# Summing the gate's four partial rows on VectorE, and issuing the queries' remainders one step later, in a one-core hybrid diffusion step

## The chip, the cores and the metric

The kernel runs on one core of a Trainium2 chip. The metric is the device time of one execution in microseconds (us). Beside the time there is a profile of one execution, taken by the hardware profiler, with a trace of every instruction.

Engines are named as in the profile: PE is TensorE (matrix products and transposes), PEld its weight loads, DVE is VectorE, ACT is ScalarE, POOL is GpSimd, SP is the engine that issues most transfers. ACT issues transfers too; in the trace those of ACT stand under ACTq, those of SP under SPq. Each engine runs its own instructions strictly in the order in which the program lists them, and waits at an instruction until all that it needs is there.

## The reference, cut to what matters

One layer of a diffusion backbone: 128 context tokens and 1024 latent tokens, width 1024. The part that the change touches is the modulation gate and the queries:

```
m = silu(cond) @ w_mod + b_mod          # cond: c for latent tokens, c_ctx for context tokens
shift, scale, gate = split(m, 3)
h = rmsnorm(x, norm_gain) * (1 + scale) + shift
q_a, k_a, v_a, g_a, q_b, k_b, v_b, g_b = split(h @ w_in)
q = rope(rmsnorm_per_head(q, qn))       # 8 heads of 64, for mixer A and for mixer B
... attention A (all keys), attention B (window of 128) ...
x = x + gate * (concat(o_a * silu(g_a), o_b * silu(g_b)) @ w_out)
```

The gate is a row of 1024 numbers for each of the two conditions. It is needed only at the very end, when the output projection is added to x.

## The kernel before, in words

All work is in tiles of 128 tokens; there are nine (the context tile is number 0). To keep fp32 accuracy, most operands are split into a high part, rounded for fast products, and a low part, the remainder (`whi`/`wlo` for weights, `qo0`/`qo1` for queries), and a product is done as three: high by high, low by high, high by low.

The order of the program is: modulation and gates of mixer A; queries of mixer A (nine blocks, `m = 0`); queries of mixer B (nine blocks, `m = 1`); keys and values (nine blocks); gates of mixer B; then attention and output, which fills the last two thirds of the time.

**A block and its steps.** A block (`block`, `project`, lines 244 to 281) is 24 products of 128x512 into one accumulation bank `pq` (or `pk` for keys): eight slices k of the width, three products each (lines 246, 247, 248, of which 247 uses the low weights `wlo`). Each block has two halves, and each half begins with a `tick()`, which runs the work that earlier blocks put in an agenda with `later(n, f)`: f runs n half blocks later. That is how the order of the work around the change is set: agenda entries of one tick run in the order in which they were put there, and every instruction then stands in its engine's list at that place.

**A query tile.** After its block, a tile goes through these steps (`query`, from line 614), at 0, 2, 3 and 6 ticks (`QUERY_AT`), for the last tile of mixer B at 0, 1, 2 and 4 (`QUERY_LAST`):

- squares: ACT squares `pq` (`sqq`, line 622), DVE sums (`ssq`, 624; `ms`, 169), POOL takes the power -1/2 (`rs`, 171);
- scale: DVE multiplies (`qnq`, 629) and makes the two rotary products (`ra`, 559; `rb`, 565);
- rotated: DVE adds them (`qfq`, 640; for tile 0 line 642);
- turned: PE transposes into a bank `ptq` (line 650; two such banks, D and E, used in turn by `bank_tr`), ACT makes the high part (`qo0q`, 653) and issues its two transfers to DRAM (`put`, 663);
- low, one tick later: DVE makes the low part (`qo1q`, 658);
- `put` of the low part, one further tick later: ACT issues two more transfers (663). There are two buffers each of `qo0` and `qo1`.

**The next weights.** During the last block of a stage, from its third slice on, the next stage's weights are split, one slice a time, the last two slices behind the block: ACT makes `whi` (line 231), DVE makes `wlo` (233). At the end of mixer A they are `whiqb`/`wloqb`, at the end of mixer B `whikv`/`wlokv`.

**The gate.** In two of mixer B's blocks (the tiles `GATE_AT`, 3 and 7 in order), `gate_rows` computes half of the gate, 512 columns: eight products over K, in four column groups of the array, so that the bank `pgate` holds four partial sums, at partitions 0, 32, 64 and 96, two rows each (one for each condition). Then ACT copies the bank to `grow` one tick later (line 604), and three ticks later `gate_sum` adds the four: PE multiplies `grow` by `sel`, a 128x2 matrix of ones and zeros, into a bank `pgs` of the D/E pair (line 593; the trace shows each such fp32 product as two), DVE adds the bias `bg` (594) and SP stores the row (595). `sel` is made once by `group_sum` (lines 320 and 322), which adds four column pairs of the identity.

Of the kernel before, what the change touches and what calls it, by code (L numbers as in the profile page):

```python
# [9 lines left out]
F32 = mybir.dt.float32  # L10
# [3 lines left out]
ALU = mybir.AluOpType  # L14
# [4 lines left out]
P = 128  # L19
# [32 lines left out]

WO_STEPS = ((0, 4, 4), (1, 5, 5), (2, 6), (3, 7), (4, 8, 6), (5, 9), (6, 11), (7, 12, 10), (8, 13), (9, 14), (10, 16))
TURN = 2
QUERY_AT = (0, 2, 3, 6)
PAD = 2
SECOND_FROM = 5
# [48 lines left out]
def hybrid_step(ctx, tc, x_prompt, x_sample, cache_k_a, cache_v_a, cache_k_b, cache_v_b,  # L106
# [3 lines left out]
    nc = tc.nc  # L110
# [13 lines left out]
    def later(n, f):  # L124

        agenda.setdefault(now[0] + n, []).append(f)
# [13 lines left out]
    def bank(tag, name):  # L140
        return ps.tile([P, 512], F32, tag=tag, name=name, bufs=BANKS[tag])

    def bank_mm(name):
        turn["mm"] += 1
        return bank(mm_tags[0][turn["mm"] % len(mm_tags[0])], name)

    def bank_tr(name):
        turn["tr"] += 1
        return bank("DE"[turn["tr"] % 2], name)
# [3 lines left out]
    ident_r = cst.tile([P, P], F32R, name="ident_r")  # L153
# [12 lines left out]
    def rsqrt_mean(pool, ss, n, width, name):  # L166

        ms = pool.tile([P, width], F32, tag="ms", name=f"ms_{name}")
        nc.vector.tensor_scalar(ms, ss, 1.0 / n, EPS, op0=ALU.mult, op1=ALU.add)  # L169
        r = pool.tile([P, width], F32, tag="rs", name=f"rs_{name}")  # L170
        nc.gpsimd.tensor_tensor(r, ms, mhalf[:, :width], op=ALU.pow)  # L171
        return r
# [136 lines left out]
    with tc.tile_pool(name="st", bufs=2, side="right") as st:  # L309
# [6 lines left out]
        nc.sync.dma_start(colt, cols)  # L316
        st.tile([P, 16], F32, name="pad3", bufs=1)

        def group_sum(out, eye):
            nc.vector.tensor_tensor(out, eye[:, 0:2], eye[:, 32:34], op=ALU.add)  # L320
            for a in (64, 96):
                nc.vector.tensor_tensor(out, out, eye[:, a : a + 2], op=ALU.add)

        wm = []

        def load_wm(j):
# [142 lines left out]
        for j in range(1, KT + 2):  # L469
# [54 lines left out]
            if KT - 2 <= j < KT:  # L524
# [3 lines left out]
                c0, n = W_QA.cols[0]  # L528
# [26 lines left out]
    def rope_products(pool, qn, nh, tab_c, tab_s, t, name, bufs=2):  # L555

        cb = tab_c[:, t - 1, :].unsqueeze(1).to_broadcast([P, nh, HD])
        ra = pool.tile([P, nh, HD], F32, tag="ra", name=f"ra_{name}", bufs=bufs)
        nc.vector.tensor_tensor(ra, qn, cb, op=ALU.mult)
        rb = pool.tile([P, nh, HD], F32, tag="rb", name=f"rb_{name}", bufs=bufs)  # L560
        rv = rb.rearrange("p h (b s f) -> p h b s f", s=2, f=16)
        qv = qn.rearrange("p h (b s f) -> p h b s f", s=2, f=16)
        sv = tab_s[:, t - 1, :].rearrange("p (b s f) -> p b s f", s=2, f=16)
        for s in range(2):
            nc.vector.tensor_tensor(rv[:, :, :, s, :], qv[:, :, :, 1 - s, :],
                                    sv[:, :, s, :].unsqueeze(1).to_broadcast([P, nh, 2, 16]), op=ALU.mult)
        return ra, rb
# [11 lines left out]
    with tc.tile_pool(name="qt", bufs=2, side="right") as qt:  # L579
# [4 lines left out]
        sil32 = qt.tile([P, KT, 32], F32, name="sil32g", bufs=1)  # L584
        nc.gpsimd.memset(sil32, 0.0)
        nc.vector.tensor_copy(sil32[:, :, 0:2], silc.rearrange("p (c k) -> p k c", c=2))
        sel = qt.tile([P, 2], F32, name="selg", bufs=1)
        group_sum(sel, ident_r.bitcast(F32))
        wg, bg = [], []

        def gate_sum(n, grow):
            pgs = bank_tr(f"pgs{n}")
            nc.tensor.matmul(pgs[0:2], sel, grow, start=True, stop=True)
            nc.vector.tensor_tensor(bg[n], pgs[0:2], bg[n], op=ALU.add)
            nc.sync.dma_start(gate_row[:, 512 * n : 512 * n + 512], bg[n])

        def gate_rows(n):
            pg = bank_mm(f"pgate{n}")
            for k in range(KT):
                a = 32 * (k % 4)  # L600
                nc.tensor.matmul(pg[a : a + 32], sil32[:, k, :], wg[2 * n + k // 4][:, k % 4, :],
                                 start=(k < 4), stop=(k >= 4), tile_position=(0, a))
            grow = qt.tile([P, 512], F32, tag="grow", name=f"grow{n}", bufs=1)
            later(1, lambda: nc.scalar.copy(grow, pg))
            later(3, lambda: gate_sum(n, grow))

        def load_wg(i):
            n, b = divmod(i, 2)
# [5 lines left out]
        def query(pq, m, t, tabs, n=1):  # L614

            nm = f"q{m}_{t}"
            pqv = pq.rearrange("p (h d) -> p h d", d=HD)
            v = {}

            def squares():  # L620
                sq = qt.tile([P, 8, HD], F32, tag="sq", name=f"sq{nm}")
                nc.scalar.activation(sq, pqv, AF.Square)  # L622
                ss = qt.tile([P, 8], F32, tag="ss", name=f"ss{nm}")
                nc.vector.tensor_reduce(ss, sq, axis=AX.X, op=ALU.add)
                v["r"] = rsqrt_mean(qt, ss, HD, 8, nm)

            def scale():
                qn = qt.tile([P, 8, HD], F32, tag="qn", name=f"qn{nm}")
                nc.vector.tensor_tensor(qn, pqv, v["r"].unsqueeze(2).to_broadcast([P, 8, HD]), op=ALU.mult)
                v["qn"] = qn  # L630
                if t:
                    v["rot"] = rope_products(qt, qn, 8, *tabs[m], t, nm)

            def rotated():

                qf = qt.tile([P, 4, 2, HD], F32, tag="qf", name=f"qf{nm}", bufs=3)
                out = qf.rearrange("p h g d -> p g h d")
                pair = lambda a: a.rearrange("p (g h) d -> p g h d", g=2)
                if t:
                    nc.vector.tensor_tensor(out, *(pair(a) for a in v["rot"]), op=ALU.add)  # L640
                else:
                    nc.vector.tensor_tensor(
                        out, pair(v["qn"]), gain4[:, 2 * m, :].unsqueeze(1).unsqueeze(1).to_broadcast([P, 2, 4, HD]),
                        op=ALU.mult)
                v["qf"] = qf

            def turned():
                ptq = bank_tr(f"pt{nm}")
                for h in range(4):
                    nc.tensor.transpose(ptq[:, P * h : P * h + P], v["qf"][:, h].rearrange("p g d -> p (g d)"),  # L650
                                        ident_r.bitcast(F32))
                qo = [qt.tile([P, 512], F32R, tag=f"qo{i}", name=f"qo{i}{nm}") for i in range(2)]
                nc.scalar.copy(qo[0], ptq)
                put(qo[0], 0)
                later(1, lambda: low(ptq, qo))

            def low(ptq, qo):
                nc.vector.tensor_tensor(qo[1], ptq, qo[0], op=ALU.subtract)
                later(1, lambda: put(qo[1], 1))

            def put(part, i):
                for g in range(2):
                    nc.scalar.dma_start(q_dram[t][m][64 * i : 64 * i + 64, 512 * g : 512 * g + 512],
                                       part[64 * g : 64 * g + 64].bitcast(F32))

            for d, f in zip(QUERY_LAST if (m, t) == (1, 0) else QUERY_AT, (squares, scale, rotated, turned)):
                later(n + d, f)

        tabs = {0: rope_tables(qt, 0, 2)}
        for m in range(2):  # L670
            w, nxt = ((W_QA, W_QB), (W_QB, W_KV))[m]
            ts = list(range(1, NT)) + [0]
            for t in ts:
                pq = bank_mm(f"pq{m}_{t}")
                if m == 1 and t in (ts[GATE_AT[0]], ts[GATE_AT[1]]):
                    gate_rows(len(wg) // 2 - 1)
                if (m, t) in ((0, ts[-2]), (1, ts[GATE_AT[0]])):
                    n = len(wg) // 2
                    load_wg(2 * n)
                    load_wg(2 * n + 1)  # L680
                    if n == 0:
                        bgt = qt.tile([34, 512], F32, name="bg", bufs=1)
                    bg.append(bgt[32 * n : 32 * n + 2])
                    nc.sync.dma_start(bg[n], b_mod[:, 2 * D + 512 * n : 2 * D + 512 * n + 512].to_broadcast([2, 512]))
                if t == ts[-2]:
                    nxt.load_all()
                    if m == 0:
                        tabs[1] = rope_tables(qt, 2, 2)
                block(pq, lambda k: project(pq, w, t, k), nxt, t == ts[-1])
                query(pq, m, t, tabs)  # L690
# [178 lines left out]
    def max_items(i):  # L869
# [19 lines left out]
        def finish():  # L889
# [10 lines left out]
            nc.vector.tensor_scalar(mn, m4, -1.0, None, op0=ALU.mult)  # L900
            later(TURN, transpose)

# [166 lines left out]
    for f in beside[2]:  # L1069
# [5 lines left out]
        name=nc.get_next_instruction_name(), engine=mybir.EngineType.Activation, act_func_set_id=6))  # L1075
# [155 lines left out]
    slots, start = [], []  # L1231
# [119 lines left out]
```

## Time and profile before

| | us |
|---|---|
| median of 3 timed runs | 716.38 (716.08 to 716.65) |
| the profiled execution, its own time | 716.94 |
| its span in the trace | 715.2 |
| PE busy | 694.4 (97%) |
| DVE busy | 463.8 (65%) |
| ACT busy | 416.4 (58%) |
| POOL busy | 334.6 (47%) |

The mean granted clock of TensorE was 0.994 of full speed. Times of events are counted from the start of the span; the execution's own time is 1.74 us more than the span, which lie around it. In the list of events in order of time, each row has the start, the time busy, engine, line, operation, what is written and read, shape and count; in brackets stands how long the engine had been idle before and what ended that. Time in which ACT issues transfers does not count as busy. Starts of products on PE lie closer together than their durations, since products overlap in the array: what a product costs is read from the distance of starts.

### The profile page before, as it was taken

The page shows a single profiled execution, that of the slowest core. Times are in us where ns is not written, and L with a number is a line of the kernel's source. Part 1 is how long each engine was busy: PE and PEld are TensorE (multiplying, and loading weights), DVE is VectorE, ACT ScalarE, POOL GpSimd, SP SyncE. Part 2 cuts the span into 40 slices and gives each one's busy share as a digit, 9 for nine tenths or more (in the row PEclk, how much of TensorE's full clock was granted, in tenths as well). Part 3 has the DMA queues.
Part 4 walks back from the last instruction along what each step waited for, and adds up shares of the span by engine and source line. Part 5 has one row for each costly group of instructions (what it writes and reads, how often), then busy time and mean ns, then how long its engine had stood idle before and what let it go on. Part 6 is the DMA issues. An engine that isn't in the chain of part 4 may idle for free. (4 is left out here: it accounts for less than half of the span.)

```text
span 715.2 us, 10633 instructions
## 1 busy us (share of the span) xinstructions
PE 694.4 (97%) x3512; PEld 559.1 (78%) x3512; DVE 463.8 (65%) x1016; ACT 416.4 (58%) x840; POOL 334.6 (47%) x356
## 2 busy tenths in 40 slices
PE   6999999999998999999999999999999999999987
PEld 4778988777686889976788888888888888887865
DVE  4767257866747864736867577567675775675662
ACT  5646411411414441178777877887788778877770
POOL 3647033232313320246757555755575557555651
PEclk9999999999999999999999999999999999999999
DMA  8962283358344026431222122122221221222323
GB/s 323 414 202 97 80 300 76 83 164 249 74 108 143 7 69 191 133 119 46 81 75 73 39 76 80 45 82 65 77 74 39 73 82 45 82 62 79 104 66 119
DMA packets 53304, 78.58 MB, mean 110 GB/s; under 512 B 6584, under 2 KB 25464, under 8 KB 52352
## 3 DMA queue, kind: packets, MB, share of 16 engines
q1 hardware_dynamic: 45072, 65.96, 28.0%
q10 hardware_dynamic: 8176, 11.94, 6.3%
q8 instruction: 28, 0.46, 0.3%
q14 instruction: 28, 0.23, 0.1%
HBM read 58.69 MB, written 19.18 MB: 109 GB/s over the span
## 5 line engine op out<-in xcount | busy, mean ns | idle before, releaser
L1136 POOL TENSOR_TENSOR pl<-pe,ph 128x512 fp32r<-128x512 f32 x130 | 167.7, 1292 | 145.4 <-DVE nm L947 67.6
L887 DVE TENSOR_REDUCE mx<-pmx 128x1 f32<-128x384 f32 x192 | 101.4, 552 | 60.2 <-PE pmx L886 58.9
L1128 ACT ACTIVATE pe<-st 128x512 f32<-128x512 f32 x146 | 86.9, 596 | 28.0 <-PE st L1126 27.0
L1132 ACT CAST ph<-pe 128x512 fp32r<-128x512 f32 x146 | 90.6, 620 | 4.8
L1146 PE MATMUL pv<-ph,v_hi 128*128 128x512 f32 x208 | 83.2, 400 | 2.2 <-DVE spare L1170 2.2
L1149 PE MATMUL pv<-pl,v_hi 128*128 128x512 f32 x208 | 82.5, 397 | 0.0
L171 POOL TENSOR_TENSOR rs_q<-ms_q,mhalf 128x8 f32<-128x8 f32 x18 | 34.8, 1931 | 82.2 <-DVE ms_q L169 82.2
L1217 PE MATMUL po<-wo,ogh 128*128 128x512 f32 x216 | 72.6, 395 | 0.2 <-DVE yt L1224 0.2
L947 DVE CUSTOM_DVE_ANT_0 sn<-sn,mask,nsink 128x512 f32<-128x512 f32 (+1 forms) x64 | 46.3, 724 | 38.4 <-PE sn L944 36.6
L886 PE MATMUL pmx<-kha,qt 128*128 128x384 f32 x192 | 60.9, 363 | 0.4 <-ACT pen L933 0.2
L1125 PE MATMUL st<-qt,kha 128*128 128x512 f32 x144 | 58.2, 404 | 1.5 <-ACT pe L1128 0.8
L1126 PE MATMUL st<-qb,kla 68*128 68x512 f32 x144 | 57.7, 401 | 1.1 <-DVE qb L906 1.1
L1148 PE MATMUL pv<-ph,v_lo 128*64 128x512 f32 x146 | 57.8, 396 | 0.0
L1149 PEld LDWEIGHTS pv<-pl,v_hi 128*128 128x128 f32 x208 | 39.3, 189 | 16.7 <-issue 0.4
L933 ACT ACTIVATE pen<-sn,nm 128x512 f32<-128x512 f32 (+2 forms) x72 | 45.1, 627 | 6.5 <-DVE nm L947 3.1
L1121 ACT CAST ph<-st 128x512 fp32r<-128x512 f32 x62 | 36.4, 588 | 19.9 <-PE st L1120 18.6
L1146 PEld LDWEIGHTS pv<-ph,v_hi 128*128 128x128 f32 x208 | 39.5, 190 | 10.7 <-ACT ogh L1182 2.4
L1217 PEld LDWEIGHTS po<-wo,ogh 128*128 128x128 f32 x216 | 39.9, 188 | 6.9 <-DVE yt L1224 0.6
L1122 DVE TENSOR_TENSOR pl<-st,ph 128x512 fp32r<-128x512 f32 x62 | 42.5, 686 | 2.1 <-ACT ph L1121 1.5
L1217 PE MATMUL po<-wo,ogl 128*128 128x512 f32 x108 | 42.5, 393 | 0.0
L622 ACT ACTIVATE sqq<-pq 128x512 f32<-128x512 f32 x18 | 10.8, 600 | 52.5 <-DMA qd<-qo0q 16.2
L886 PEld LDWEIGHTS pmx<-kha,qt 128*128 128x128 f32 x192 | 35.5, 190 | 6.3 <-DVE mx L887 1.4
(219 smaller groups left out, 1700.7 us busy)
## 6 DMA issues: line engine op xcount, KB each, us to landing
qt<-qd SPq DMA_DIRECT2D x36, 256.0 KB, 3.0
wm<-in_w_mod_ss_dram SPq DMA_DIRECT2D x7, 1024.0 KB, 10.0
qd<-qo0q ACTq DMA_DIRECT2D x36, 128.0 KB, 2.4
qd<-qo1q ACTq DMA_DIRECT2D x36, 128.0 KB, 2.4
sgl<-gd SPq DMA_DIRECT2D x36, 128.0 KB, 2.1
out_dram<-yt SPq DMA_DIRECT2D x17, 256.0 KB, 2.1
xn<-in_x_sample_dram SPq DMA_DIRECT2D x8, 512.0 KB, 6.1
wg<-in_w_mod_g_dram SPq DMA_DIRECT2D x4, 1024.0 KB, 8.4
```

Of the source, the lines that this page charges most:

```text
L886: nc.tensor.matmul(pm[:, 0:384], lhs, kha[:, g, 3 * b : 3 * b + 3, :], start=True, stop=True)
L887: nc.vector.tensor_reduce(mx[:, h, b : b + 1], pm[:, 0:384], axis=AX.X, op=ALU.max)
L947: nc.vector.tensor_tensor_reduce(s, s, mask[:, m0 : m0 + n], -1.0, nsink[:, 4 * g + h : 4 * g + h + 1], op0=ALU.add, op1=ALU.min, accum_ou ...
L1125: nc.tensor.matmul(s, kh, qtile[i], start=True, stop=False)
L1126: nc.tensor.matmul(s, kl, qbtile[i], start=False, stop=True)
L1128: nc.scalar.activation(pe, s, AF.Exp)
L1132: nc.scalar.copy(ph, pe)
L1136: nc.gpsimd.tensor_tensor(pl, pe, ph, op=ALU.subtract)
L1146: nc.tensor.matmul(pv, two, ph, start=(b == 0), stop=False)
L1148: nc.tensor.matmul(pv[0:64, :], vl, ph, start=False, stop=False)
L1149: nc.tensor.matmul(pv, two, pl, start=False, stop=last)
L1217: nc.tensor.matmul(po[n], a, wo_parts[KT * n + k][lo], start=(k == KS[0] and p == 0), stop=(k == KS[-1] and p == 2))
```

## The change

Two things. First, the product with `sel` goes, with `sel`, `grow`, ACT's copy and the extra bank: one tick after the gate's products, four DVE additions of 2x512 add the partial rows to the bias straight from the bank `pgate`, at partitions 0, 32, 64 and 96, each into `bg`. SP's store follows as before. Second, a new constant `PUT_LOW = 2` moves the transfers of a query's low part one tick later.

```
+PUT_LOW = 2
...
-        def group_sum(out, eye):
-            nc.vector.tensor_tensor(out, eye[:, 0:2], eye[:, 32:34], op=ALU.add)
-            for a in (64, 96):
-                nc.vector.tensor_tensor(out, out, eye[:, a : a + 2], op=ALU.add)
...
-        sel = qt.tile([P, 2], F32, name="selg", bufs=1)
-        group_sum(sel, ident_r.bitcast(F32))
         wg, bg = [], []

-        def gate_sum(n, grow):
-            pgs = bank_tr(f"pgs{n}")
-            nc.tensor.matmul(pgs[0:2], sel, grow, start=True, stop=True)
-            nc.vector.tensor_tensor(bg[n], pgs[0:2], bg[n], op=ALU.add)
+        def gate_sum(n, pg):
+            for a in range(0, P, 32):
+                nc.vector.tensor_tensor(bg[n], pg[a : a + 2], bg[n], op=ALU.add)
             nc.sync.dma_start(gate_row[:, 512 * n : 512 * n + 512], bg[n])
...
-            grow = qt.tile([P, 512], F32, tag="grow", name=f"grow{n}", bufs=1)
-            later(1, lambda: nc.scalar.copy(grow, pg))
-            later(3, lambda: gate_sum(n, grow))
+            later(1, lambda: gate_sum(n, pg))
...
             def low(ptq, qo):
                 nc.vector.tensor_tensor(qo[1], ptq, qo[0], op=ALU.subtract)
-                later(1, lambda: put(qo[1], 1))
+                later(PUT_LOW, lambda: put(qo[1], 1))
```

ACT's list at the end of mixer B's queries, from tile 4's transposed query to the third slice of the key weights, before. A name's first number is the query's tile, the last number only tells instances apart; `qd` is the queries' place in DRAM:

```order
L653 CAST qo0q_4_2024<-ptq_4_2019 128x512
L663 DMA qd_1_66<-qo0q_4_2024 64x512 x2
L663 DMA qd_1_64<-qo1q_3_1936 64x512 x2
L622 ACTIVATE sqq_7_2038<-pq_7_1929 128x512
L604 COPY grow_1994<-pgate_1985 128x512
L653 CAST qo0q_5_2080<-ptq_5_2075 128x512
L663 DMA qd_1_68<-qo0q_5_2080 64x512 x2
L663 DMA qd_1_66<-qo1q_4_2025 64x512 x2
L622 ACTIVATE sqq_8_2098<-pq_8_1984 128x512
L231 CAST whikv_2115<-rawkv_1995 128x512
L231 CAST whikv_2122<-rawkv_1998 128x512
L231 CAST whikv_2132<-rawkv_2001 128x512
```

The same place in the changed kernel (its lines are numbered up to nine lower behind the gate's functions, so the squares' line 622 is 613 there):

```order
L644 CAST qo0q_4_2018<-ptq_4_2013 128x512
L654 DMA qd_1_66<-qo0q_4_2018 64x512 x2
L613 ACTIVATE sqq_7_2030<-pq_7_1924 128x512
L654 DMA qd_1_64<-qo1q_3_1931 64x512 x2
L644 CAST qo0q_5_2078<-ptq_5_2073 128x512
L654 DMA qd_1_68<-qo0q_5_2078 64x512 x2
L613 ACTIVATE sqq_8_2090<-pq_8_1979 128x512
L232 CAST whikv_2107<-rawkv_1989 128x512
L232 CAST whikv_2114<-rawkv_1992 128x512
L654 DMA qd_1_66<-qo1q_4_2019 64x512 x2
L232 CAST whikv_2126<-rawkv_1995 128x512
```

The squares of a tile now stand ahead of the transfers of an earlier tile's low part, the copy to `grow` is gone, and two transfers stand between the second and the third slice of the key weights. The same swap of squares and transfers is in every query block from tile 5 of mixer A on, and the end of mixer A has the same place between `whiqb` slices two and three. Behind the query of tile 7 of mixer B the two lists are the same.

DVE's list at the second half of the gate, before:

```order
L624 TENSOR_REDUCE ssq_7_2040<-sqq_7_2038 128x8
L169 TENSOR_SCALAR ms_q_7_2042<-ssq_7_2040 128x8
L640 TENSOR_TENSOR qfq_6_2059<-ra_q_6_2031,rb_q_6_2033 128x2x4x64
L658 TENSOR_TENSOR qo1q_4_2025<-ptq_4_2019,qo0q_4_2024 128x512
L629 TENSOR_TENSOR qnq_7_2085<-pq_7_1929,rs_q_7_2044 128x512
L559 TENSOR_TENSOR ra_q_7_2087<-qnq_7_2085,tcos_1437 128x512
L565 TENSOR_TENSOR rb_q_7_2089<-qnq_7_2085,tsin_1439 128x16x16 x2
L594 TENSOR_TENSOR bg<-pgs_2092,bg 2x512
L624 TENSOR_REDUCE ssq_8_2100<-sqq_8_2098 128x8
L169 TENSOR_SCALAR ms_q_8_2102<-ssq_8_2100 128x8
L233 TENSOR_TENSOR wlokv_2116<-rawkv_1995,whikv_2115 128x512
L233 TENSOR_TENSOR wlokv_2123<-rawkv_1998,whikv_2122 128x512
```

and in the changed kernel:

```order
L615 TENSOR_REDUCE ssq_7_2032<-sqq_7_2030 128x8
L170 TENSOR_SCALAR ms_q_7_2034<-ssq_7_2032 128x8
L587 TENSOR_TENSOR bg<-pgate_1980,bg 2x512 x4
L631 TENSOR_TENSOR qfq_6_2055<-ra_q_6_2025,rb_q_6_2027 128x2x4x64
L649 TENSOR_TENSOR qo1q_4_2019<-ptq_4_2013,qo0q_4_2018 128x512
L620 TENSOR_TENSOR qnq_7_2083<-pq_7_1924,rs_q_7_2036 128x512
L555 TENSOR_TENSOR ra_q_7_2085<-qnq_7_2083,tcos_1433 128x512
L561 TENSOR_TENSOR rb_q_7_2087<-qnq_7_2083,tsin_1435 128x16x16 x2
L615 TENSOR_REDUCE ssq_8_2092<-sqq_8_2090 128x8
L170 TENSOR_SCALAR ms_q_8_2094<-ssq_8_2092 128x8
L234 TENSOR_TENSOR wlokv_2108<-rawkv_1989,whikv_2107 128x512
L234 TENSOR_TENSOR wlokv_2115<-rawkv_1992,whikv_2114 128x512
```

One addition behind `rb_q_7` has become four ahead of `qfq_6`, all still ahead of the low parts of the key weights. On PE the only difference is that the two rows `pgs<-grow,selg` are gone; since they no longer take a bank of the D/E pair, each transposed query now follows its predecessor into the other bank. SP's list is the same.

## The prediction

> **What bounds the kernel now.** I read the page first, then who waits for whom on PE in the query and key stages, then the events of PE, ACT and DVE there in order of time. The page's head:
>
> ```profile
> span 715.2 us, 10633 instructions
> PE 694.4 (97%) x3512; PEld 559.1 (78%) x3512; DVE 463.8 (65%) x1016; ACT 416.4 (58%) x840; POOL 334.6 (47%) x356
> ```
>
> PE sets the time. In the stretch from 85 to 260 us (queries, keys, first gates of B), where all of the change lies, PE's waits are these four, with total, count and longest in us:
>
> ```profile
> PE ptk L755 <- DVE klp L773: 1.4, 1, 1.4
> PE ptk L755 <- ACT k2k L749: 1.1, 1, 1.1
> PE ptq L650 <- DVE qo1q L658: 0.5, 1, 0.5
> PE pq L247 <- DVE wloqb L233: 0.3, 1, 0.3
> ```
>
> So here a product taken off PE is time off the kernel, as long as DVE and ACT still deliver ahead of PE. PE's events show what a product of the gate sum costs, as the distance between transposes of queries (`ptq`), one per block:
>
> ```profile
> 134.16 0.60 PE L650 MATMUL ptq<-ident_r,qfq 128*128 128x128 f32 x4
> 140.66 0.60 PE L650 MATMUL ptq<-ident_r,qfq 128*128 128x128 f32 x4
> ...
> 160.45 0.60 PE L650 MATMUL ptq<-ident_r,qfq 128*128 128x128 f32 x4
> 161.11 1.02 PE L593 MATMUL pgs<-grow,selg 128*2 128x512 f32 x2
> 167.64 0.60 PE L650 MATMUL ptq<-ident_r,qfq 128*128 128x128 f32 x4
> ...
> 187.43 0.60 PE L650 MATMUL ptq<-ident_r,qfq 128*128 128x128 f32 x4
> 188.07 1.02 PE L593 MATMUL pgs<-grow,selg 128*2 128x512 f32 x2
> 195.22 0.63 PE L650 MATMUL ptq<-ident_r,qfq 128*128 128x128 f32 x4 [0.46 <-DVE qo1q L658]
> 195.91 0.39 PE L247 MATMUL pk<-wlokv,h 128*128 128x512 f32 x1
> 200.70 0.39 PE L247 MATMUL pk<-wlokv,h 128*128 128x512 f32 x1
> 201.16 0.60 PE L650 MATMUL ptq<-ident_r,qfq 128*128 128x128 f32 x4
> 207.09 1.03 PE L650 MATMUL ptq<-ident_r,qfq 128*128 128x128 f32 x8
> ```
>
> A block without anything else takes 207.09 - 201.16 = 5.93 us. Three blocks take longer, and each is a term of the sum.
>
> **The first gate sum on PE.** 167.64 - 160.45 = 7.19 us, 1.26 more than a plain block. No wait stands there, so the product costs 1.26, and that goes. (The row of the product alone has 1.02; the rest is the change from one kind of product to another, and I take the block's difference, since PE's ends are modelled.)
>
> **The second gate sum on PE.** 195.22 - 187.43 = 7.79, which is 1.86 more: 1.26 for the product, and the rest for the wait of 0.46. That wait is for a bank: `pgs` took the turn of one of the two transpose banks, so `ptq` of tile 6 got the bank of tile 5, whose low part DVE makes only here:
>
> ```profile
> 194.39 0.68 DVE L658 TENSOR_TENSOR qo1q<-ptq,qo0q 128x512 fp32r<-128x512 f32 x1
> ```
>
> Without `pgs`, tile 6 gets the bank of tile 4, whose low part is a block older. So up to 1.86 goes.
>
> **Remainders one step later.** At the end of mixer A, 140.66 - 134.16 = 6.50, 0.57 more than plain. There PE waits for the third low slice of mixer B's weights:
>
> ```profile
> 124.74 2.09 ACTq L663 DMA_DIRECT2D qd<-qo1q  x2
> 126.88 0.60 ACT L622 ACTIVATE sqq<-pq 128x512 f32<-128x512 f32 x1 [3.37 <-issue]
> 127.51 0.69 DVE L624 TENSOR_REDUCE ssq<-sqq 128x8 f32<-128x512 f32 x1 [1.72 <-ACT sqq L622]
> 135.94 3.68 DVE L233 TENSOR_TENSOR wloqb<-rawqb,whiqb 128x512 fp32r<-128x512 f32 x6
> 136.67 0.50 PE L247 MATMUL pq<-wloqb,h 128*128 128x512 f32 x1 [0.28 <-DVE wloqb L233]
> ```
>
> The low slices are late because DVE is late, and DVE is late because it sat idle for 1.72 us until ACT's squares of tile 7, which stood behind 2.09 us of issuing transfers. With the squares ahead of those transfers, DVE starts 1.72 us earlier here, and 0.45 is enough (PE would have been there at 136.22). So 0.57 goes. The two transfers now stand between the second and third high slice on ACT; by the rows of mixer B's end below they take 1.2 us, and ACT makes the third high slice about 2 us before DVE takes it, so that costs nothing.
>
> In all other blocks PE does not wait for the queries' steps: `ptq` comes three ticks behind `qfq`, about 9 us. There the swap moves ACT and DVE only. The low part's buffer is written again two blocks later, and its transfers now have one tick (3 us) less to land; they still have a block and a half.
>
> **Where the gain can be eaten: DVE at the second gate.** I keep the clock of before up to `ptq` of tile 5 (187.43), as if the shift so far were nil; all there hangs on PE and moves with it. ACT:
>
> ```profile
> 182.14 0.59 ACT L653 CAST qo0q<-ptq 128x512 fp32r<-128x512 f32 x1 [4.26 <-PE ptq L650]
> 182.76 1.10 ACTq L663 DMA_DIRECT2D qd<-qo0q  x2
> 183.96 1.20 ACTq L663 DMA_DIRECT2D qd<-qo1q  x2
> 185.21 0.60 ACT L622 ACTIVATE sqq<-pq 128x512 f32<-128x512 f32 x1 [2.48 <-DMA qd<-qo0q]
> ...
> 189.88 1.21 ACTq L663 DMA_DIRECT2D qd<-qo1q  x2
> 191.13 0.60 ACT L622 ACTIVATE sqq<-pq 128x512 f32<-128x512 f32 x1 [2.48 <-DVE rb_q L565]
> 191.63 4.25 ACT L231 CAST whikv<-rawkv 128x512 fp32r<-128x512 f32 x8
> ```
>
> and DVE:
>
> ```profile
> 185.84 0.69 DVE L624 TENSOR_REDUCE ssq<-sqq 128x8 f32<-128x512 f32 x1 [2.40 <-ACT sqq L622]
> ...
> 188.86 0.69 DVE L629 TENSOR_TENSOR qnq<-pq,rs_q 128x512 f32<-128x512 f32 x1 [0.93 <-POOL rs_q L171]
> ...
> 190.19 0.75 DVE L565 TENSOR_TENSOR rb_q<-qnq,tsin 128x256 f32<-128x256 f32 x2
> 190.98 0.68 DVE L594 TENSOR_TENSOR bg<-pgs,bg 2x512 f32<-2x512 f32 x1
> 191.76 0.69 DVE L624 TENSOR_REDUCE ssq<-sqq 128x8 f32<-128x512 f32 x1
> ...
> 192.56 1.30 DVE L233 TENSOR_TENSOR wlokv<-rawkv,whikv 128x512 fp32r<-128x512 f32 x2
> ...
> 194.99 3.69 DVE L233 TENSOR_TENSOR wlokv<-rawkv,whikv 128x512 fp32r<-128x512 f32 x6
> ...
> 204.80 0.68 DVE L642 TENSOR_TENSOR qfq<-qnq,gain 128x512 f32<-128x512 f32 x1
> ```
>
> The squares of tile 7 (185.21) go ahead of 1.2 us of transfers, so they start at 183.92 and DVE's sum at 184.55, 1.29 earlier. Then four additions instead of one. The changed kernel's addition is not in the trace; the nearest row is the present one, also 2x512 from a bank: 0.68 long, and 191.76 - 190.98 = 0.78 from its start to the next. Each of the four needs the one before, so they can't overlap: I take 4 x 0.78 = 3.12. The lower end is 4 x 0.60, the distance of DVE's independent operations ((3.69 - 0.68)/5 in the row at 194.99); an upper end of 1.0 each allows for a wait between them that no row has. What the additions push away is covered in part: POOL's 0.93 is now over while they run. So the first low slice of the key weights moves by -1.29 + 3.12 - 0.78 - 0.93 = +0.12, to 192.68, and the third from 194.99 to 195.11. PE used a slice 0.73 after DVE had begun it (136.67 - 135.94), so the third is there for PE at 195.84.
>
> On this point the Trainium skill has a rule that speaks against the change. "VectorE: DVE Perf Modes", section "Two Vector instructions with no wait between them", says that an instruction whose operand starts in another group of 32 partitions than its predecessor's is held until everything ahead has finished. The addition at 190.98, with its bias at partition 32, agrees: it began 0.04 after the end of the one before (190.19 + 0.75), and the next 0.10 after its own end. Without such holding, and without the dependence, the sum would take the 0.60 and lose nothing at PE.
>
> PE, without `pgs`, has `ptq` of tile 6 at 187.43 + 5.93 = 193.36, its first low key product at 194.05 (0.69 later, as 195.91 stands to 195.22), and one slice each 0.684 ((200.70 - 195.91)/7), so it wants the third low slice at 195.42. It waits 0.42; the wait at mixer A's end cost 0.12 more than its 0.45, so I take 0.54. DVE then does a slice in 0.60 and PE one in 0.684, so later slices are in time. The high slices stand at 190.4 to 191.4 (two), then 1.2 us of transfers, then from 192.7: 2.4 us ahead of the third low one. What is left of 1.86 is 1.32.
>
> DVE's next deadline is `qfq` of tile 0, which moves with the low slices to 204.92, done 205.60; PE, at 193.36 + 0.54 + 5.94 + 5.93 = 205.77 for tile 8 and 0.35 later for tile 0, just does not wait. From there ACT's and DVE's lists are the old ones, and all hangs on these transposes, so the two waits for keys (1.4 and 1.1) stay and move along. The gate's first half on DVE has the same 3.12 - 0.78 more, but no weights behind it; DVE's idle time takes it (2.40 us in one block, by the row at 185.84), and without that it would cost at most those 2.34. SP's store of the gate row comes earlier, and with it the key weights' loads queued behind it. ACT's copies, 0.58 each, and the making of `sel`, were hidden; they give nothing.
>
> **Sum.** 1.26 + 1.32 + 0.57 = 3.15 us. The profiled execution's 716.94 would become 713.8; the median of the runs shown is 0.56 lower, 716.38, so I forecast a median of 713.2. If the additions took 0.60 each, nothing would be lost at PE: 3.69, 712.7. At 1.0 each, 0.88 more is lost: 2.27, 714.1.
>
> **Rivals.** (1) *The key weights become the bound more strongly*: the additions cost over 1.0 each, or a transfer's wait between the second and third high slice holds ACT. At 1.25 each the gain is 3.15 - 1.88 = 1.3, 715.1. For it: four dependent operations at just this place, with 0.4 already missing. Against: no DVE row of this size takes over 0.8. Chance 0.12, a sixth of it within 0.2%. (2) *The chain to the first keys does not follow*: ACT sends the last low parts behind a buffer that must land first,
>
> ```profile
> 211.37 5.06 ACTq L663 DMA_DIRECT2D qd<-qo1q  x6
> ```
>
> and PE waits for what comes behind. If that chain hangs on DVE instead of PE's last transposes, the 1.32 is given back as a longer wait for keys: 1.83 left, 714.6; if it hangs on landings alone, nearly all is lost. Against: in the lists its first link is the transpose of tile 8. Chance 0.08, half of it within 0.2%. (3) *Slower*: the moved transfers need a free place in the transfer queue. Ahead of the third high slice they would block ACT, then DVE, then PE. Six of them took 5.06 above, against 3.6 at 0.6 each, so about 1.4 of stall is seen. The margin there is the 2.4 less 0.5 that the slice itself takes; to undo 3.15 and add 1.43 (0.2%) the stall would have to exceed 6.5 us, which gives 717.8 or more. Nothing like it is in the trace. Chance 0.04. My forecast, a gain of 2.3 to 3.7, keeps 0.76.
>
> **Numbers.** A measurement of this kernel can tell about 0.2%, 1.43 us. Faster: 0.76 + 0.10 + 0.04 = 0.90, of which I keep 0.89 for what I have not seen; same 0.07; slower 0.04. The range goes from the full 3.69 with the runs' spread of 0.3 below (712.4) to rival 2's 714.6 with 0.2 above (714.8).
>
> **What would show it.** Right: no `pgs` on PE; plain blocks of 5.93 at 160 and at the end of mixer A; the first wait of PE behind mixer B's queries a third low key slice of 0.3 to 0.5; four additions 0.72 to 0.80 apart; the waits for keys still near 1.1 and 1.4. Wrong: additions at 1 us or more, ACT stalled between the second and third `whikv`, or waits for keys that have grown by what was gained.

## The result and the profile after

The changed kernel takes 713.00 us, the median of 6 runs (711.86 to 714.28); the kernel before 716.23 (6 runs, 715.53 to 716.65). The ratio is 0.9956, with a 95% interval of 0.9943 to 0.9970: 3.2 us faster. The profiled execution took 713.77 us against 716.94. The runs of the changed kernel spread by 2.4 us. The granted clock is one reason, since it was 1.00 in the four runs up to 713.58 and 0.994 to 0.995 in the two slowest; it is not the only one, since the four at 1.00 still lie 1.72 us apart. So in all that follows I compare the stretch in which the change lies, where the clock was 1.00 in every profile, and not single times.

The page's head after:

```profile
span 711.9 us, 10620 instructions
PE 692.2 (97%) x3508; PEld 559.0 (79%) x3508; DVE 467.4 (66%) x1019; ACT 415.4 (58%) x838; POOL 334.6 (47%) x356
```

The span is 3.3 us shorter and PE does 2.2 us less (four product instructions are gone); DVE does 3.6 us more and is still only 66% busy. PE's waits between 85 and 260 us, with total, count and longest:

```profile
PE ptk L746 <- DVE klp L764: 1.5, 1, 1.5
PE ptk L746 <- ACT k2k L740: 0.9, 1, 0.9
```

The two waits for the first keys are the old ones (1.4 and 1.1 before). The waits for `qo1q` and for mixer B's low slices are gone, and nothing of 0.3 or more has come in their place. PE's events in order of time, transposes of queries (`ptq`), some low key products, and the first transposes of keys (`ptk`):

```profile
134.22 0.60 PE L641 MATMUL ptq<-ident_r,qfq 128*128 128x128 f32 x4
140.15 0.60 PE L641 MATMUL ptq<-ident_r,qfq 128*128 128x128 f32 x4
...
159.94 0.60 PE L641 MATMUL ptq<-ident_r,qfq 128*128 128x128 f32 x4
165.88 0.60 PE L641 MATMUL ptq<-ident_r,qfq 128*128 128x128 f32 x4
...
185.67 0.60 PE L641 MATMUL ptq<-ident_r,qfq 128*128 128x128 f32 x4
191.60 0.60 PE L641 MATMUL ptq<-ident_r,qfq 128*128 128x128 f32 x4
...
192.98 0.39 PE L248 MATMUL pk<-wlokv,h 128*128 128x512 f32 x1
...
193.85 0.50 PE L248 MATMUL pk<-wlokv,h 128*128 128x512 f32 x1
...
197.82 0.60 PE L641 MATMUL ptq<-ident_r,qfq 128*128 128x128 f32 x4
...
203.76 1.17 PE L641 MATMUL ptq<-ident_r,qfq 128*128 128x128 f32 x8
...
219.48 0.66 PE L746 MATMUL ptk<-ident_r,k2k 128*128 128x128 f32 x4 [0.92 <-ACT k2k L740]
```

Distances between transposes are the blocks, and a block without anything else is 5.93 us:

| block | before | after | change | predicted |
|---|---|---|---|---|
| end of mixer A | 6.50 | 5.93 | -0.57 | -0.57 |
| first gate half | 7.19 | 5.94 | -1.25 | -1.26 |
| second gate half | 7.79 | 5.93 | -1.86 | -1.86 |
| first keys, where the third low slice comes | 5.94 | 6.22 | +0.28 | +0.54 |
| sum | | | -3.40 | -3.15 |

Two low key products are 0.68 us apart where nothing waits; here the second to third are 0.87, and this is the wait that was forecast, at half the size; at 0.19 us it is not printed as a wait. The eight transposes at 203.76 come 3.33 earlier than before (207.09); the difference from 3.40 is that the changed kernel's queries began 0.06 later. From there to the first key transpose it is 15.72 us in both kernels (219.48 less 203.76, and before 222.81 less 207.09), and behind the keys the two run alike. The row of before:

```profile
222.81 0.66 PE L755 MATMUL ptk<-ident_r,k2k 128*128 128x128 f32 x4 [1.06 <-ACT k2k L749]
```

DVE at the second gate half, the four additions in one row (`bg<-pgate,bg`), then the first and the third low slices (`wlokv`):

```profile
182.78 0.69 DVE L615 TENSOR_REDUCE ssq<-sqq 128x8 f32<-128x512 f32 x1 [2.16 <-ACT sqq L613]
183.50 0.17 DVE L170 TENSOR_SCALAR ms_q<-ssq 128x8 f32<-128x8 f32 x1
183.71 2.85 DVE L587 TENSOR_TENSOR bg<-pgate,bg 2x512 f32<-2x512 f32 x4
186.58 0.69 DVE L631 TENSOR_TENSOR qfq<-ra_q,rb_q 128x512 f32<-128x512 f32 x1
...
187.91 0.68 DVE L620 TENSOR_TENSOR qnq<-pq,rs_q 128x512 f32<-128x512 f32 x1
...
190.70 1.29 DVE L234 TENSOR_TENSOR wlokv<-rawkv,whikv 128x512 fp32r<-128x512 f32 x2
...
193.12 3.69 DVE L234 TENSOR_TENSOR wlokv<-rawkv,whikv 128x512 fp32r<-128x512 f32 x6
```

From the first addition to what follows it are 186.58 - 183.71 = 2.87 us, so one addition takes 0.72. POOL's wait ahead of `qnq` (0.93 before) is covered by them, as forecast. ACT at the same place; rows with ACTq are issues of transfers:

```profile
182.15 0.60 ACT L613 ACTIVATE sqq<-pq 128x512 f32<-128x512 f32 x1 [1.18 <-issue]
182.23 1.18 ACTq L654 DMA_DIRECT2D qd<-qo1q  x2
...
188.07 0.60 ACT L613 ACTIVATE sqq<-pq 128x512 f32<-128x512 f32 x1 [1.18 <-issue]
188.20 0.47 ACTq L654 DMA_DIRECT2D qd<-qo1q  x1
188.57 1.13 ACT L232 CAST whikv<-rawkv 128x512 fp32r<-128x512 f32 x2
189.26 0.45 ACTq L654 DMA_DIRECT2D qd<-qo1q  x1
189.75 3.22 ACT L232 CAST whikv<-rawkv 128x512 fp32r<-128x512 f32 x6
```

The squares wait 1.18 us for the issuing of one pair of transfers instead of 2.48 for two. The other pair is issued while the squares and the first slices are worked on.

### The profile page after: what moved, and what is told of

The parts are those of the page before. It is cut to its first block, busy times and chain, and to the rows that moved or that the text cites. A ratio compares the mean times of both kernels' runs of the same rounds, so it can differ in the third digit from the quotient of the medians.

```text
span 711.9 us, 10620 instructions
## 1 busy us (share of the span) xinstructions
PE 692.2 (97%) x3508; PEld 559.0 (79%) x3508; DVE 467.4 (66%) x1019; ACT 415.4 (58%) x838; POOL 334.6 (47%) x356
## 5 line engine op out<-in xcount | busy, mean ns | idle before, releaser
L644 ACT CAST qo0q<-ptq 128x512 fp32r<-128x512 f32 x18 | 10.6, 587 | 59.6 <-PE ptq L641 58.3
```

## The experiments

My theory is the sum of the prediction: PE got back two products and their turns in the transpose banks, and the wait for weights at the end of mixer A, and pays a smaller new wait at the key weights; the transfers one step later are what lets DVE bear the additions. The rivals named with each run give another split of the 3.4 us. Each kernel is read by one stretch: from a query transpose of mixer A at 104 us to the key transpose that follows `ptc`, one ahead of all blocks that changed and one behind them.

| kernel | time, us | from | to | stretch | against after |
|---|---|---|---|---|---|
| before | 716.94 | 104.53 | 237.25 | 132.72 | +3.36 |
| after | 713.77 | 104.60 | 233.96 | 129.36 | |
| gate alone | 715.10 | 104.26 | 235.33 | 131.07 | +1.71 |
| transfers alone | 716.62 | 104.13 | 235.44 | 131.31 | +1.95 |
| bank turn | 715.01 | 104.39 | 235.51 | 131.12 | +1.76 |
| more additions | 715.99 | 104.06 | 234.89 | 130.83 | +1.47 |
| late additions | 714.54 | 104.08 | 233.38 | 129.30 | -0.06 |
| third buffer | 712.62 | 104.21 | 233.17 | 128.96 | -0.40 |
| both | 712.68 | 104.18 | 232.88 | 128.70 | -0.66 |

The times are those of the profiled executions. Behind the stretch the spans have 479.3 to 479.4 us left in "transfers alone", "more additions" and "late additions", whose granted clock between 305 and 325 us was 0.83. In all others it is 477.6 to 478.0; their clock there was 0.91 (before, after, "both") or 1.00. This difference, which lies outside the stretch, is the main reason why the table's times and stretches are not in the same order.

**Gate alone.** The changed kernel with the transfers of the low part where they were:

```
-PUT_LOW = 2
+PUT_LOW = 1
```

> The changed kernel with PUT_LOW = 1, so the four additions alone. Theory (the parts work together): the last block of mixer A, to mixer B's first transpose, takes 6.50 us again instead of 5.93, and at the second gate the squares stand behind 1.2 us of transfers again, so DVE reaches the third low key slice about 1.29 later and PE waits there for 1.5 in place of 0.3. Span about 713.7 (before 715.2, changed 711.9). Rival (the parts just add up, and the moved transfers are worth only the 0.57 of mixer A): span about 712.5.

The gain over before is 1.65 us. PE around the second gate half:

```profile
185.73 0.60 PE L641 MATMUL ptq<-ident_r,qfq 128*128 128x128 f32 x4
191.67 0.60 PE L641 MATMUL ptq<-ident_r,qfq 128*128 128x128 f32 x4
...
195.22 0.50 PE L248 MATMUL pk<-wlokv,h 128*128 128x512 f32 x1 [0.76 <-DVE wlokv L234]
199.21 0.60 PE L641 MATMUL ptq<-ident_r,qfq 128*128 128x128 f32 x4
```

The gate half itself is a plain block (5.94), but the block with the first keys has grown to 7.54, 1.60 over plain: PE now waits for the first low key slice (0.31) and for the third (0.76, above), and most of the 1.86 goes back. DVE's sum of squares explains it:

```profile
184.15 0.69 DVE L615 TENSOR_REDUCE ssq<-sqq 128x8 f32<-128x512 f32 x1 [2.24 <-ACT sqq L613]
```

PE's transpose at 185.73 stands where it stood in the changed kernel (185.67), so this is 1.31 us later than there (184.15 - 182.78, less 0.06). The low slices follow it. So the transfers are what pays for the additions at this gate. The stretch is 1.71 longer than the changed kernel's, where the theory has 1.8 and the rival 0.6.

**Transfers alone.** The kernel before with the low parts' transfers one step later, and its products kept:

```
+PUT_LOW = 2
...
-                later(1, lambda: put(qo[1], 1))
+                later(PUT_LOW, lambda: put(qo[1], 1))
```

> The kernel before with the low part's transfers one tick later, the gate sum on PE as before. Theory: 0.57 at the end of mixer A, and, since DVE starts its work at the second gate 1.29 earlier, the low part of tile 5 is there when tile 6 wants its bank: the 0.46 wait with its 0.13 goes too. Blocks with a gate sum stay at 7.2. Span about 714.0. Rival (the bank's wait hangs on the gate's own work): only 0.57, span 714.6.

The gain is 1.41 us, more than both numbers. PE's transposes and products at the two gate halves:

```profile
159.48 0.60 PE L651 MATMUL ptq<-ident_r,qfq 128*128 128x128 f32 x4
160.01 1.02 PE L594 MATMUL pgs<-grow,selg 128*2 128x512 f32 x2
166.54 0.60 PE L651 MATMUL ptq<-ident_r,qfq 128*128 128x128 f32 x4
...
186.33 0.60 PE L651 MATMUL ptq<-ident_r,qfq 128*128 128x128 f32 x4
...
193.39 0.60 PE L651 MATMUL ptq<-ident_r,qfq 128*128 128x128 f32 x4
```

Both gate blocks are 7.06 long, not 7.19 and 7.79. At the second half 0.73 has gone, and at the first 0.13. The product follows the transpose by 0.53 here and by 0.66 before (161.11 - 160.45), so 0.13 of what I had called the product's cost was a wait of the product itself. A row of before fits its bank:

```profile
187.24 0.69 DVE L658 TENSOR_TENSOR qo1q<-ptq,qo0q 128x512 fp32r<-128x512 f32 x1
```

This low part ended at 187.93, 0.14 ahead of the product at 188.07. No wait is printed there, as it is so short. So one product costs PE 7.06 - 5.93 = 1.13 us, the turn 0.13 at each half and 0.60 more at the second; with mixer A's end (139.69 less 133.75, both `ptq` rows of this kernel, is 5.94) the transfers alone give 0.56 + 0.13 + 0.73 = 1.42. The two parts of the change alone give 1.65 + 1.41 = 3.06, together 3.36, so only 0.30 needs both.

**A bank turn without the product.** The changed kernel, in which each gate half skips one turn of the two transpose banks, at the step at which the product used to take it:

```
             later(1, lambda: gate_sum(n, pg))
+            later(3, lambda: turn.update(tr=turn["tr"] + 1))
```

> The changed kernel, but three ticks after each gate the turn of the two transpose banks is stepped once without use, as the product's bank did. Theory: at the second gate the transpose of tile 6 gets tile 5's bank and waits until its low part is made (192.5 to 193.2 in the changed kernel, PE there at 191.6): block 1.65 longer, the wait of 0.28 for the key slice gone, span 713.3. Rival (the wait of before belonged to the product, not to the bank's turn): span 711.9.

```profile
185.73 0.60 PE L642 MATMUL ptq<-ident_r,qfq 128*128 128x128 f32 x4
193.41 0.63 PE L642 MATMUL ptq<-ident_r,qfq 128*128 128x128 f32 x4 [1.58 <-DVE qo1q L650]
```

The second gate half takes 7.68 us, 1.75 over plain, with no product in it: PE stands 1.58 for the low part whose bank it was handed. The stretch loses 1.76: the next block gains 0.27, since it no longer waits for the third key slice, and the blocks ahead of this half take 0.27 more than in the changed kernel, 0.17 of it at the first half, where the turn is skipped too. Before, product and wait together cost 1.86 here. The 0.11 between the two is not the product's: tile 5's low part begins 6.85 us behind its transpose here (192.58 less 185.73) and began 6.96 behind it before (194.39 less 187.43). So before, the product lay wholly inside time that the bank cost anyway. By these rows, taking away the product alone and keeping its turn would have brought next to nothing at this half; no run has just that.

**More additions.** The changed kernel with an unread tile `extra`, into which DVE makes four further additions at the first half and two at the second; the output is not touched:

```
             for a in range(0, P, 32):
                 nc.vector.tensor_tensor(bg[n], pg[a : a + 2], bg[n], op=ALU.add)
+            for a in (32, 64, 96, 32)[: 4 - 2 * n]:
+                nc.vector.tensor_tensor(extra[32 * n : 32 * n + 2], pg[a : a + 2], bg[n], op=ALU.add)
```

> The changed kernel with more DVE work of the same kind behind the additions, into a tile that nobody reads: four more 2x512 additions at the first gate, two more at the second. Theory: at 0.72 each, the four at the first gate cost PE nothing, the two at the second make PE wait 1.4 longer for the third low key slice; span 713.3. Rival (DVE's idle time covers both): 711.9. Rival (DVE's work counts everywhere): 716.2.

```profile
159.41 0.60 PE L645 MATMUL ptq<-ident_r,qfq 128*128 128x128 f32 x4
165.34 0.60 PE L645 MATMUL ptq<-ident_r,qfq 128*128 128x128 f32 x4
...
191.07 0.60 PE L645 MATMUL ptq<-ident_r,qfq 128*128 128x128 f32 x4
198.73 0.60 PE L645 MATMUL ptq<-ident_r,qfq 128*128 128x128 f32 x4
```

At the first half, eight additions cost PE nothing: the block is 5.93. At the second, two more lengthen the block with the first keys from 6.22 to 7.66, by 1.44, which is twice 0.72. So there every microsecond that is added on DVE is one of PE, and at the first half none is. The stretch is 1.47 longer, as the theory has it (1.4); the rivals have 0 and 4.3.

**Late additions.** The changed kernel with the second half's additions eight steps later, behind the key weights:

```
-            later(1, lambda: gate_sum(n, pg))
+            later(9 if n else 1, lambda: gate_sum(n, pg))
```

> The changed kernel with the second gate's four additions nine ticks behind the gate's products instead of one, so behind all low key slices and behind the query of tile 0, where DVE sat idle for 1.9 us. Theory: PE's wait for the third low key slice, 0.28 in the block's length, goes; the low part of tile 8, which then stands behind the additions, is not on the path to the keys; span 711.6. Rival (the additions then delay the chain to the first keys): PE's waits for keys grow from 2.4 by up to 2 us, span 712 to 714.

```profile
191.09 0.60 PE L641 MATMUL ptq<-ident_r,qfq 128*128 128x128 f32 x4
197.02 0.60 PE L641 MATMUL ptq<-ident_r,qfq 128*128 128x128 f32 x4
202.96 1.04 PE L641 MATMUL ptq<-ident_r,qfq 128*128 128x128 f32 x8
218.92 0.66 PE L746 MATMUL ptk<-ident_r,k2k 128*128 128x128 f32 x4 [1.31 <-ACT k2k L740]
```

The wait for the third slice has gone: the block is 5.93 instead of 6.22. But the stretch is only 0.06 shorter. From the eight transposes to the first key it is now 15.96 us, 0.24 more than the 15.72. ACT's own row there:

```profile
204.21 1.34 ACTq L654 DMA_DIRECT2D qd<-qo0q  x2
```

and in the changed kernel:

```profile
205.01 1.10 ACTq L654 DMA_DIRECT2D qd<-qo0q  x2
```

The same two issues took 1.10 there, and 0.24 is the difference. The late additions run beside them; why the issue is longer is not settled. What was won at one place was lost at the next, on ACT.

**A third buffer for the low parts.** The changed kernel:

```
-                qo = [qt.tile([P, 512], F32R, tag=f"qo{i}", name=f"qo{i}{nm}") for i in range(2)]
+                qo = [qt.tile([P, 512], F32R, tag=f"qo{i}", name=f"qo{i}{nm}", bufs=2 + i) for i in range(2)]
```

> The changed kernel with three buffers instead of two for the low parts of queries. Theory on PE's two remaining waits for keys (0.92 and 1.47): they come from DVE waiting 4.5 us, until the low part of tile 7 has landed, to reuse its buffer for tile 0; with a third buffer the last six transfers take about 3.6 instead of 5.07 us, ACT comes to the keys 1.4 earlier, and PE's waits shrink by about as much in total: span 710.5. Rival (the first keys hang on the landing of the last transfers or on PE's own blocks): span 711.9.

ACT's last transfers and first work on keys, in the changed kernel and in this one:

```profile
208.03 5.07 ACTq L654 DMA_DIRECT2D qd<-qo1q  x6
...
215.19 0.37 ACT L771 CAST v_hi<-pk 128x256 fp32r<-128x256 f32 x1 [1.66 <-DMA qd<-qo1q]
```

```profile
207.73 3.86 ACTq L654 DMA_DIRECT2D qd<-qo1q  x6
...
214.43 0.37 ACT L771 CAST v_hi<-pk 128x256 fp32r<-128x256 f32 x1 [2.40 <-DMA qd<-qo1q]
```

and PE's first key transpose in this one:

```profile
218.72 0.65 PE L746 MATMUL ptk<-ident_r,k2k 128*128 128x128 f32 x4 [0.50 <-ACT k2k L740]
```

Issuing takes 3.86 instead of 5.07, so the stall of 1.2 us for a buffer was real and is gone. But `v_hi`, whose place the queries' tiles held until then, now waits 2.40 instead of 1.66 for the landing of the same transfers. Between 195 and 225 us the low parts' transfers took a median of 2.8 us from issue to landing, at most 3.1, against 2.4 and 2.4 in the changed kernel. So less is left: PE gets its key 0.46 us earlier counted from its transposes at 203.46 (15.26 instead of 15.72). It is mostly the rival: the landing holds the keys, and the issue only a third. (The span, 710.8, looks like the theory's 710.5, but of its 1.1 less than the changed kernel's only 0.4 lies in the stretch; 0.4 is an earlier start and 0.3 lies behind.)

**Both.** The last two edits together:

> Late additions at the second gate and the third buffer together. Theory: both gains add up, 0.3 and 1.4: span about 710.2, time 0.6 to 0.75% below the kernel before, against 0.44% for the changed kernel. Rival (the late additions fall into the time that the third buffer wins): span 711 to 712.

The first key comes 15.34 us behind the eight transposes (218.40 less 203.06), between the two alone (15.96 and 15.26); the two issues on ACT that took 1.34 in "late additions" took 1.20 here. A median of 712.73 us (5 runs, 712.26 to 713.04) against 717.12 for the kernel before beside it (9 runs, 715.46 to 717.86): a ratio of 0.9939, interval 0.9926 to 0.9953. Its stretch is 0.66 shorter than the changed kernel's. That is more than the 0.46 of the two edits alone, but far from the 1.7 that the theory added up, and within what the rival leaves (0 to 0.9), though the ratio just reaches the 0.6% that the theory named. Its interval overlaps with that of the changed kernel (0.9943 to 0.9970), so by time alone the two are not told apart; by the stretch it is the best of all.

## Why the prediction was right

**PE sets the time.** Right: 3.40 us fewer in four of PE's blocks became 3.36 in the stretch and 3.3 in the span. Nothing is left over for ACT's copies, as forecast.

**The products.** Both blocks lost just what was forecast (1.25 and 1.86), but I had split it wrongly. A product costs 1.13; 0.13 of each 1.26 was its own wait for a transpose bank, and with the transfers moved that would have gone without the product, as "transfers alone" shows. What I had called the change from one kind of product to another is then 1.13 less 1.02, and that is not looked into. The bank's part of 1.86 is larger than the 0.46 printed as a wait: alone, it costs 1.75 ("bank turn"). The costs overlap and do not add, so that the total of 1.86 was right and its two parts were not.

**The additions on DVE.** This is the term that was mis-sized: 0.54 lost at PE was forecast, 0.28 measured. The squares came at 182.15, where the prediction put them (183.92 on the old clock, less the 1.76 by which PE was ahead). Four additions take 2.87, not 3.12. The 0.78 that I had taken for one was too long, because the row behind it was waiting: there the addition ended at 191.66 (190.98 + 0.68), the next tile's squares on ACT at 191.73 (191.13 + 0.60), and `ssq` began at 191.76. Where `ssq` is printed as waiting for the squares, at 185.84, it too begins 0.03 after their end. With what they cost at their edges, from the start of `ssq` to that of `qnq` without POOL's wait, it is 5.13 - (3.02 - 0.93) = 3.04. The old addition at its other place was worth more than 0.78: from `rb_q` to `ssq` it is now 0.67 (189.24 to 189.91), and was 1.57 (190.19 to 191.76), so 0.90. Sum: 1.20 instead of 1.41 from `ssq` to the first low slice, and the third slice came at 193.12, 0.23 earlier than forecast. PE used it 0.73 after, as it did the slice from which I took that number. The first rival is this same term, too small instead of too large; "more additions" shows that its price was right (1.44 of PE for 1.44 of DVE) and that only the durations that it needed are not there.

The rule that I had cited from the Trainium skill ("VectorE: DVE Perf Modes", section "Two Vector instructions with no wait between them") agrees with the edges: at the first half, whose row of the bias lies at partition 0, the first addition begins 0.09 ahead of the end of `ms_q`, and at the second, at partition 32, 0.04 behind it:

```profile
157.78 0.17 DVE L170 TENSOR_SCALAR ms_q<-ssq 128x8 f32<-128x8 f32 x1
157.86 2.83 DVE L587 TENSOR_TENSOR bg<-pgate,bg 2x512 f32<-2x512 f32 x4
```

The 0.10 behind the old addition, which I had also read as the rule, is no sign of it, since `ssq` waited for the squares there. Within the four, dependence and holding can't be told apart, since each needs the one before. The four further additions of "more additions" at the first half don't need each other's result, though they write the same two rows, and they begin 0.71 to 0.73 us apart as well (160.19, 160.90, 161.62, 162.35). So needing each other's result is not what sets the distance; whether holding or the shared target does, no run separates.

**Remainders one step later.** Right in size (0.57 at mixer A's end) and in its cause: without it 0.40 of the 0.57 comes back there (6.33 between the transposes of "gate alone" at 133.88 and 140.21; the two transfers ahead of the squares took 1.78 us to issue there, and 2.09 before), and at the second gate half it is worth 1.31 us of DVE, against 1.29 forecast. I had taken it that the two transfers between the second and third high slice cost ACT 1.2 us. They cost 0.12: the first two slices took 1.13 from 188.57, and the third began at 189.75 instead of 188.57 + 2 x 0.53 = 189.63 (0.53 being an eighth of the 4.25 before). DVE never waited for it. In "transfers alone" the third slice stood 0.35 for an issue (its row is at 190.71), and DVE still never waited. So the third rival, ACT stalled in the moved transfers, has nothing for it. The stall of 1.4 that it read in the last six transfers was mostly the wait for a buffer of the low parts, since 1.2 of it went with a third buffer, and so not for a place in a queue. An issue can be held for another reason too: the two at 124.74 before took 2.09 us, though DVE had made their data by 122.79 (122.10 + 0.69); what held them no run shows, and between the two slices nothing like it came.

**The chain to the first keys.** Right: 15.72 us from the eight transposes in both. In the changed kernel the eight took 0.14 longer (1.17 against 1.03), so "just does not wait" was a little too good; the keys did not feel it. The second rival did not come true for this change, but the chain has little to spare: in "late additions" 0.24 of the 0.29 won ahead of it was lost again on ACT, and in "third buffer" 0.46 of the 1.2 won at the issues reached PE.

**The time.** The sum gave 713.8 for the profiled execution, and it took 713.77; this is closer than its terms are, and so partly luck, since PE's blocks gave 0.25 more, and the later start (0.06) and the time around the span (1.87 against 1.74) took back most of it.

## What to carry to other kernels

A small product that borrows a turn of a rotating bank can cost its own time (1.13 us here) or the longer wait of the bank's next taker (up to 1.86), and the two overlap: look at what the next taker of the bank waits for before counting either. Work put on an engine that is a third idle is free or fully paid by place: here eight additions cost nothing at one gate half, and at the other two more than the four cost PE their whole 1.44 us, because weights with a deadline stood behind them. When transfers are issued on an engine that also computes, the piece of work for which another engine waits goes ahead of them.

## What the runs showed of the chip

- ACT issues transfers ahead of arithmetic that its list has before them, so "strictly in the order" of the opening section is too strict for it. Transfers that stand behind the squares in ACT's list were issued 0.08 us after the squares began (182.15 and 182.23), and the next pair, which stands behind two slices, began at 188.20, ahead of both (188.57). The other way round nothing overlaps: squares behind a pair of transfers waited 1.18 us for their issue. So a transfer ahead of a computation cost its whole issue of 0.5 to 0.6 us there, and one behind a computation little: the slice that followed the pair lost 0.12 us in the changed kernel and 0.35 in "transfers alone".
- One core alone, with nearly the same instructions, was granted a clock of 0.83, 0.91 or 1.00 between 305 and 325 us from one profile to the next, always one of these three. The work behind the stretch took 479.3 to 479.4 us in the three profiles with 0.83 and 477.6 to 478.0 in the six others, with no difference between 0.91 and 1.00 that stands out. The runs of the changed kernel spread by 2.4 us; a difference of less than that is better read from a stretch of the trace.
